# Storing gated convolution pieces one piece later in the out stage of a hybrid decoder layer

## The chip, the cores and the metric

The kernel runs on one core of a Trainium2 chip. The metric is the device time of one execution in microseconds (us). Five engines of the core matter here: PE (TensorE, matrix products), DVE (VectorE), ACT (ScalarE), POOL (GpSimd) and SP, whose queue issues most of the DMAs of this stage. Each works through its own list of instructions in order; an instruction whose data isn't ready holds everything behind it on that engine.

## The reference

One decoder layer is applied to a prompt of 2048 tokens and to 8 samples of 4 tokens. The input is normalised and projected, and its columns go to four groups of heads, each 512 wide; the outputs, gated, are concatenated, projected by `w_out` (2048 to 1024), normalised and added to the input.

```python
def conv_branch(a, b, hist, w_dw, b_dw, ln_g, ln_b, w_pw, b_pw):
    u = a * jax.nn.sigmoid(b)
    y = depthwise_conv31(concat([hist, u]), w_dw) + b_dw
    y = jax.nn.silu(layer_norm(y, ln_g, ln_b))
    y = y @ w_pw + b_pw                      # this step and the gate are
    ...                                      # what the change touches
y = concat([y_c * silu(gate_c), y_pool * ..., y_sb * ..., y_mem * ...]) @ w_out
out = x + rms_norm(y, post_g)
```

The other groups are a multi-scale pooling mixer, a stick-breaking attention (which for the samples reads a paged cache of 8192 tokens) and an attention over 256 memory tokens.

## The kernel before

The change lies in the last stage, "out", from about 1986 us to the end. Two streams of work are woven together there.

The first is the projection by `w_out`, made as seven Strassen-like products of half-size matrices in a fixed list (1, 7, then 2 and 6 mixed, then 4, 5 and 3). Each product has nine parts (eight of 256 tokens' worth of columns and one for the samples), each part two halves `h`. Both operands are fp32 split into a high and a low fp32r half, so a step takes three matmuls: `wohi` with `mh`, `wohi` with `ml`, `wolo` with `mh` (L1881, tile `acc`; 1408 matmuls in all). `out_part` yields after every quarter part. The right operand is read back from the mixture in DRAM (`mixd` for the prompt, `mixs` for the samples; loads `mr` at L1593 and L1610), combined on POOL (L1623), split on ACT (`mh`, L1635) and on DVE (`ml`, L1646). The weights are loaded raw (`wor`, L1514 and L1526), combined on POOL (L1536), written back to scratch for a later product (`wsd`, L1531) and split on ACT (`wohi`, L1542) and DVE (`wolo`, L1547). A finished `acc` is added into running sums on DVE (`U`, L1680 and L1681; `c`, L1684).

The second stream, `conv_post`, is the end of the convolution group. It takes the depthwise output in 8 blocks of 256 tokens (the last has 288, with the 32 sample tokens) and is a generator with these steps per block:

- `load` reads `cy`; `total` sums its four tiles on POOL (`cs`, L1372).
- `center`: PE makes the mean (`cm`, L1377), DVE subtracts it (L1380), ACT squares (`csq`, L1382), POOL adds the four squares (L1384).
- `scale`: PE makes the variance (`cv`, L1390), ACT and DVE its inverse root; for two tiles at a time DVE normalises (`ct`, L1399), ACT takes the sigmoid (`csg`, L1402), DVE multiplies (L1406), ACT and DVE split into `shi` (L1408) and `slo` (L1411).
- `gate` loads a gate piece into `cgt` (L1418), four pieces of 128 channels per block, three buffers.
- `point`, per piece: 12 matmuls `cz` (L1432) into one of two PSUM buffers, DVE's `cgt` = (cz + bias) * gate (L1435), and SP's store of the piece to `mixd` (L1437), for the last block also to `mixs` (L1439).

The main body steps `conv_post` once per 0.9 quarter parts (`OPACE`). After each block's pieces a flag ("conv", i) tells the other stream that its rows of the mixture may be read. Before it loads the weights of product 4, whose buffers lie in the convolution's memory, the main body runs `conv_post` to its end at one place of the list. PE's list is in program order; the lists of DVE, ACT, POOL and SP are ordered by a scheduler from the program's dependencies and so change with it.

## Time and profile before

| | |
|---|---|
| median of 3 runs | 2420.67 us (2417.32 to 2421.38) |
| profiled execution | 2424.11 us, span 2422.4 us |
| mean granted TensorE clock | 0.981 |
| PE busy | 2288.3 us, 94% of the span |
| DVE busy | 1720.1 us, 71% |
| POOL busy | 1301.5 us, 54% |
| ACT busy | 1116.8 us, 46% |
| bytes moved by DMA | 562.14 MB, mean 232 GB/s |

Busy is the share of the span in which an engine executes. In the lines of the profile shown below, a row of the timeline gives the start in us, the duration in us, engine, line, operation, output tile <- input tiles, partitions x elements with the type, and in brackets how long the engine had been idle and what released it. A row of the waits gives the waiting instruction, the releaser, the sum of the waits in us, their number and the longest. "SPq" is SP's queue of DMA issues; its row stands at the time of issue. "x2" behind a row means that two like instructions are merged in it.

### The profile page before, as it was taken

The numbers are of one execution on the slowest core, as the hardware profiler recorded it, in microseconds if no ns is written. First come the engines' busy times: TensorE is split into PE (matmuls) and PEld (weight loads), VectorE is DVE, ScalarE is ACT, GpSimd is POOL, SyncE is SP. The second block draws the span as 40 slices with busy tenths as digits, with TensorE's granted clock in tenths as the row PEclk, the third lists the DMA queues.
The fourth block names the chain that finished last, engine by engine and source line by source line (L and its number), as shares of the span: only waits on it lengthen the run. The fifth ranks groups of instructions, "written<-read, shape, count | busy, mean of one in ns | idle before, by whom it ended". The sixth has DMA issues, their size and how long they took to land. (4 is left out here: it accounts for less than half of the span.)

```text
span 2422.4 us, 42131 instructions
## 1 busy us (share of the span) xinstructions
PE 2288.3 (94%) x15962; PEld 1777.0 (73%) x15962; DVE 1720.1 (71%) x2410; ACT 1116.8 (46%) x1939; POOL 1301.5 (54%) x1333
## 2 busy tenths in 40 slices
PE   6999999999999999999999999899999998989997
PEld 6998888898888777777777776455555556778775
DVE  5333684968746665477777877888898846787898
ACT  5322343242442322224242425788989955443454
POOL 1553544555564455655555564576876845453431
PEclk9999999999999999999999999999999998999998
DMA  5678988877778799887877876834332227887764
GB/s 184 196 254 284 344 303 285 295 263 264 268 244 282 268 349 327 312 280 265 286 272 268 266 245 153 246 85 119 101 85 74 66 61 237 263 275 255 248 237 171
DMA packets 340438, 562.14 MB, mean 232 GB/s; under 512 B 28482, under 2 KB 212930, under 8 KB 323835
## 3 DMA queue, kind: packets, MB, share of 16 engines
q1 hardware_dynamic: 284858, 290.72, 39.1%
q0 software_dynamic: 55376, 268.72, 31.1%
q8 instruction: 126, 2.06, 0.3%
q14 instruction: 78, 0.63, 0.1%
HBM read 469.28 MB, written 90.68 MB: 231 GB/s over the span
## 5 line engine op out<-in xcount | busy, mean ns | idle before, releaser
L925 DVE STREAM_TRANSPOSE T<-kt 128x1024 f32<-128x1024 f32 x256 | 308.7, 1225 | 184.7 <-PE sSA L938 172.3
L892 POOL DMA_INDIRECT vt<-in_cache_v_dram,idv x256 | 251.3, 982 | 243.3 <-PE sO L977 182.3
L583 DVE SCALAR_TENSOR_TENSOR cacc<-U,par,cacc 128x512 f32<-128x512 f32 x480 | 360.0, 750 | 11.8
L1277 POOL TENSOR_TENSOR be<-be,E 128x512 f32<-128x512 f32 (+2 forms) x320 | 303.3, 955 | 115.4 <-DVE E L1268 49.4
L1268 DVE TENSOR_TENSOR_SCAN E<-gam,cr,ZM 128x513 f32<-128x513 f32 x192 | 232.8, 1262 | 15.3 <-ACT gam L1253 14.1
L892 POOL DMA_INDIRECT kt<-in_cache_k_dram,idk x128 | 125.6, 981 | 201.5 <-DVE T L925 141.0
L1288 PEld LDWEIGHTS AT<-ident,be 128*128 128x128 f32 x1088 | 116.7, 141 | 127.4 <-ACT at L1294 45.3
L1253 ACT ACTIVATE gam<-S,nbias_bc 128x1024 f32<-128x1024 f32 (+1 forms) x160 | 172.6, 1079 | 49.4 <-issue 18.5
L1881 PE MATMUL acc<-wohi,mh 128*128 128x512 f32 (+1 forms) x480 | 194.3, 405 | 0.9 <-ACT mh L1635 0.9
L1881 PE MATMUL acc<-wolo,mh 128*128 128x512 f32 (+1 forms) x480 | 190.9, 398 | 0.0
L1881 PE MATMUL acc<-wohi,ml 128*128 128x512 f32 x448 | 179.1, 400 | 10.0 <-DVE ml L1646 9.9
L1248 PE MATMUL S<-kT,Q 128*128 128x512 f32 (+1 forms) x640 | 176.4, 399 | 6.9 <-ACT be L1255 2.6
L1255 ACT ACTIVATE be<-S,bias_bc 128x1024 f32<-128x1024 f32 (+1 forms) x160 | 171.5, 1072 | 0.0
L1288 PE MATMUL AT<-ident,be 128*128 128x128 f32 x1088 | 157.0, 282 | 14.4 <-DVE at L1292 3.9
L1304 PE MATMUL av<-at,V 128*64 128x512 f32 (+3 forms) x640 | 152.6, 555 | 1.7 <-DVE sbo L1309 1.7
L938 PE MATMUL sSA<-T,W 128*32 128x128 f32 x4096 | 139.2, 277 | 6.8 <-DVE T L925 6.0
L938 PEld LDWEIGHTS sSA<-T,W 128*32 128x32 f32 x4096 | 104.7, 110 | 44.1 <-issue 37.4
L1646 DVE TENSOR_TENSOR ml<-mr,mh 128x512 fp32r<-128x512 f32 x108 | 100.2, 933 | 36.8 <-ACT mh L1635 36.6
L977 PE MATMUL sO<-vt,saT 128*32 128x512 f32 x1024 | 124.0, 598 | 0.0
L1248 PEld LDWEIGHTS S<-kT,Q 128*128 128x128 f32 x640 | 106.1, 194 | 23.2 <-ACT gam L1253 4.2
L1265 DVE TENSOR_TENSOR_SCAN E<-gam,ZM 128x128 f32<-128x128 f32 (+3 forms) x128 | 96.3, 801 | 29.6 <-ACT gam L1253 23.3
L1294 ACT COPY at<-AT 128x512 f32<-128x512 f32 x192 | 109.0, 656 | 14.4 <-PE AT L1288 14.4
(571 smaller groups left out, 6047.2 us busy)
## 6 DMA issues: line engine op xcount, KB each, us to landing
Q<-qd SPq DMA_DIRECT2D x64, 256.0 KB
mr<-mixd SPq DMA_DIRECT2D x32, 512.0 KB
mr<-mixd SPq DMA_DIRECT2D x48, 256.0 KB
wor<-in_w_out_dram SPq DMA_DIRECT2D x20, 512.0 KB
xtp<-in_x_prompt_dram SPq DMA_DIRECT2D x16, 512.0 KB
kT<-kd SPq DMA_DIRECT2D x64, 128.0 KB
wor<-in_w_out_dram SPq DMA_DIRECT2D x32, 256.0 KB
msd<-mr SPq DMA_DIRECT2D x32, 256.0 KB
```

Source lines behind the costliest of these rows:

```text
L583: dve.scalar_tensor_tensor(out=ps, in0=U[:, a + k : a + k + H], scalar=wd[:, k : k + 1], in1=ps, op0=ALU.mult, op1=ALU.add)
L892: pool.indirect_dma_start(out=dst, out_offset=None, in_=rows, in_offset=bass.IndirectOffsetOnAxis(ap=idx, axis=0))
L925: dve.transpose(T[:, 2 * hh : 2 * hh + 2].rearrange("p s j t -> p (s j t)"), kt[:, 2 * hh : 2 * hh + 2].rearrange("p s j d -> p (s j d)"))
L938: pe.matmul(sSs[n][32 * g : 32 * g + 32, P * ml : P * (ml + 1)], lhsT=W[:, jj, :], rhs=T[:, :, jj, :], start=i == 0, stop=i == 3, tile_pos ...
L1248: pe.matmul(S[:, j, :w], lhsT=Q[hh][:, x, P * (q2 + j) : P * (q2 + j + 1)], rhs=KT[hp, hh, kc][:, :w], start=x == 0, stop=x == 1)
L1253: act.activation(out=ga[:, :, 512 - w : 512], in_=S[:, :, :w], func=AF.Sigmoid, bias=nbias_bc[:, h : h + 1], scale=-1.0)
L1255: act.activation(out=be[:, :, :w], in_=S[:, :, :w], func=AF.Sigmoid, bias=bias_bc[:, h : h + 1])
L1268: dve.tensor_tensor_scan(out=E[:, j][:, ::-1], data0=ga[:, j][:, ::-1], data1=ZM[:, 0:1].to_broadcast([P, 513]), initial=carry[hh, q2][:, ...
L1277: pool.tensor_tensor(out=be[:, j, :m], in0=be[:, j, :m], in1=E[:, j, 513 - w : 513 - w + m], op=ALU.mult)
L1288: pe.transpose(ap_[:, P * qt : P * (qt + 1)], A[hp, qb, kc, hh, qt][:, P * r : P * (r + 1)], ident)
L1304: pe.matmul(av[64 * hh : 64 * hh + 64, c], lhsT=V[:, 4 * kc + r, 64 * hh : 64 * hh + 64], rhs=ats.pop((hp, qb, kc, r, hh))[:, c], start=dg ...
L1881: pe.matmul(o[:rows], lhsT=m[a][:, k, :rows], rhs=W[prod, 4 * h + k][w], start=not cont and h == k == n == 0, stop=h == 1 and k == 3 and n ...
```

## The change

Three things change in `conv_post`.

A piece's store isn't issued behind its own gating any more. It is put in a list `gated`, and `send(1)`, one turn of the generator after the piece, issues all but the newest; the block's last store is issued by `send(0)` behind the piece loop. The gate pieces get five buffers for three, in the pool `cpw`.

The additions of squares leave `center` for a step `squares`, at the seventh of the eleven turns between a block's start and its pieces.

Behind the pieces of a block, the first segment of the next block's `scale` (the matmul `cv`, the root and its inverse) is taken at once, followed by two more turns, and only then are the last store and the flag issued. A block so takes one turn more, 28 for 27.

```diff
--- before.py
+++ after.py
@@ -1356,7 +1356,11 @@
 
         CW = CB + NS
         blocks = [(a, a + CB) for a in range(0, SEQ - CB, CB)] + [(SEQ - CB, SEQ + NS)]
-        ys, sums, sqs, split, gates = {}, {}, {}, {}, {}
+        ys, sums, sqs, split, gates, gated = {}, {}, {}, {}, {}, []
+
+        def send(keep_):
+            while len(gated) > keep_:
+                wq.dma_start(*gated.pop(0))
 
         def load(i):
             if i < len(blocks):
@@ -1380,9 +1384,14 @@
                 dve.tensor_tensor(out=y[:, c, :N], in0=y[:, c, :N], in1=mps[:, :N], op=ALU.subtract)
                 sq.append(cp.tile([P, CW], F32, tag="csq", name=f"csq{a0}_{c}", bufs=4)[:, :N])
                 act.activation(out=sq[c], in_=y[:, c, :N], func=AF.Square)
-            for a, b in ((0, 1), (2, 3), (0, 2)):
-                pool.tensor_tensor(out=sq[a], in0=sq[a], in1=sq[b], op=ALU.add)
-            sqs[i] = sq[0]
+            sqs[i] = sq
+
+        def squares(i):
+            if i in sqs:
+                sq = sqs[i]
+                for a, b in ((0, 1), (2, 3), (0, 2)):
+                    pool.tensor_tensor(out=sq[a], in0=sq[a], in1=sq[b], op=ALU.add)
+                sqs[i] = sq[0]
 
         def scale(i):
             a0, N, y = blocks[i][0], blocks[i][1] - blocks[i][0], ys.pop(i)
@@ -1414,7 +1423,7 @@
 
         def gate(i, co):
             a0, a1 = blocks[i]
-            gates[i, co] = cp.tile([P, CW], F32, tag="cgt", name=f"cgt{a0}_{co}", bufs=3)
+            gates[i, co] = cpw.tile([P, CW], F32, tag="cgt", name=f"cgt{a0}_{co}", bufs=5)
             wq.dma_start(gates[i, co][:, : a1 - a0], gcd[co, :, a0:a1])
 
         def point(i):
@@ -1434,12 +1443,12 @@
                         n += 1
                 dve.scalar_tensor_tensor(out=g[:, :N], in0=ps[:, :N], scalar=par[:, co, CONV_K + 3 : CONV_K + 4],
                                          in1=g[:, :N], op0=ALU.add, op1=ALU.mult)
-                wq.dma_start(mix_rows(co, a0, CB), by_tile(g[:, :CB]))
+                gated.append((mix_rows(co, a0, CB), by_tile(g[:, :CB])))
                 if N > CB:
-                    wq.dma_start(mixs[0, :, co], g[:, CB:N])
-                yield
-                yield
-            flags.add(("conv", i))
+                    gated.append((mixs[0, :, co], g[:, CB:N]))
+                yield
+                send(1)
+                yield
 
         load(0)
         load(1)
@@ -1464,6 +1473,7 @@
             yield
             yield
         total(1)
+        squares(0)
         for _ in scale(0):
             yield
         for _ in range(4):
@@ -1474,11 +1484,18 @@
             if i + 1 < len(blocks):
                 center(i + 1)
                 side = scale(i + 1)
-            for _ in range(D2):
+            for k in range(D2):
+                if k == 6:
+                    squares(i + 1)
                 yield
             for _ in point(i):
                 yield
             total(i + 2)
+            next(side, None)
+            yield
+            yield
+            send(0)
+            flags.add(("conv", i))
             for _ in side:
                 yield
             for _ in range(D1):
```

What this does to the lists of the engines is shown at three places. A name as `wor_4` is a raw weight tile, `mr_1_0` a raw tile of the mixture (part 1, half 0), `cgt_2` gated piece 2; the number behind it is the build's own. Line numbers of the changed kernel are 4 to 17 above those of the kernel before; a store of a piece stands at L1363 there.

SP's list around the stores of the first block, before:

```order
L1437 DMA mixd<-cgt_0_20194 128x2x128
L1514 DMA wor_4_20218<-in_w_out_dram 128x2x512
L1514 DMA wor_5_20257<-in_w_out_dram 128x2x512
L1437 DMA mixd<-cgt_1_20281 128x2x128
L1418 DMA cgt_3_20343<-gcd 128x256
L1437 DMA mixd<-cgt_2_20312 128x2x128
L1593 DMA mr_0_0_20382<-mixd 128x2x512
L1593 DMA mr_0_1_20440<-mixd 128x2x512
L1437 DMA mixd<-cgt_3_20343 128x2x128
L1531 DMA wsd<-wor_4_20218 128x512
L1593 DMA mr_1_0_20473<-mixd 128x2x512
L1531 DMA wsd<-wor_5_20257 128x512
```

and now:

```order
L1531 DMA wor_4_20215<-in_w_out_dram 128x2x512
L1363 DMA mixd<-cgt_0_20194 128x2x128
L1531 DMA wor_5_20257<-in_w_out_dram 128x2x512
L1427 DMA cgt_3_20342<-gcd 128x256
L1363 DMA mixd<-cgt_1_20281 128x2x128
L1610 DMA mr_0_0_20380<-mixd 128x2x512
L1363 DMA mixd<-cgt_2_20311 128x2x128
L1363 DMA mixd<-cgt_3_20342 128x2x128
L1610 DMA mr_0_1_20430<-mixd 128x2x512
L1548 DMA wsd<-wor_4_20215 128x512
L1610 DMA mr_1_0_20473<-mixd 128x2x512
L1548 DMA wsd<-wor_5_20257 128x512
```

The raw weight 4 now stands ahead of the store of piece 0. The store of piece 3 follows the store of piece 2, and the second read of the mixture, `mr_0_1`, has moved behind it. Behind these rows follow, in both, the raw weight 6, a gate piece and the raw weight 7.

SP's list around the last block's stores, before:

```order
L1437 DMA mixd<-cgt_2_22197 128x2x128
L1439 DMA mixs<-cgt_2_22197 128x32
L1526 DMA wor_0_22303<-in_w_out_dram 128x512
L1526 DMA wor_0_22303<-wsd 128x512
L1437 DMA mixd<-cgt_3_22215 128x2x128
L1439 DMA mixs<-cgt_3_22215 128x32
L1526 DMA wor_1_22306<-in_w_out_dram 128x512
L1526 DMA wor_1_22306<-wsd 128x512
L1610 DMA mr_7_1_22294<-mixd 128x512
L1526 DMA wor_2_22328<-in_w_out_dram 128x512
L1686 DMA c11d<-c_5_22290 128x512
```

and now:

```order
L1363 DMA mixd<-cgt_0_22153 128x2x128
L1363 DMA mixs<-cgt_0_22153 128x32
L1363 DMA mixd<-cgt_1_22179 128x2x128
L1363 DMA mixs<-cgt_1_22179 128x32
L1363 DMA mixd<-cgt_2_22196 128x2x128
L1363 DMA mixs<-cgt_2_22196 128x32
L1363 DMA mixd<-cgt_3_22214 128x2x128
L1363 DMA mixs<-cgt_3_22214 128x32
L1627 DMA mr_7_1_22294<-mixd 128x512
L1543 DMA wor_0_22303<-in_w_out_dram 128x512
L1543 DMA wor_0_22303<-wsd 128x512
L1543 DMA wor_1_22306<-in_w_out_dram 128x512
```

The first raw weights of product 4 (`wor_0`, one half from the input and one from scratch) stood ahead of the store of piece 3; now they stand behind all eight stores and behind the read `mr_7_1`.

DVE's list in the last block, from the second half of `scale` to the first gating, before:

```order
L1406 TENSOR_SCALAR ct_0_22047<-ct_0_22047,par,csg_0_22049 128x288
L1406 TENSOR_SCALAR ct_1_22051<-ct_1_22051,par,csg_1_22053 128x288
L1411 TENSOR_TENSOR slo_22046<-ct_0_22047,shi_22045 128x288
L1411 TENSOR_TENSOR slo_22046<-ct_1_22051,shi_22045 128x288
L1399 TENSOR_SCALAR ct_2_22078<-cy_21590,par,cv_22038 128x288
L1399 TENSOR_SCALAR ct_3_22082<-cy_21590,par,cv_22038 128x288
L1646 TENSOR_TENSOR ml_5_1_22150<-mr_5_1_22057,mh_5_1_22149 128x512
L1406 TENSOR_SCALAR ct_2_22078<-ct_2_22078,par,csg_2_22080 128x288
L1406 TENSOR_SCALAR ct_3_22082<-ct_3_22082,par,csg_3_22084 128x288
L1680 TENSOR_TENSOR U_20001<-acc_4_22131,U_20001 128x512
L1411 TENSOR_TENSOR slo_22046<-ct_2_22078,shi_22045 128x288
L1411 TENSOR_TENSOR slo_22046<-ct_3_22082,shi_22045 128x288
```

and now:

```order
L1697 TENSOR_TENSOR U_19998<-acc_4_22123,U_19998 128x512
L1415 TENSOR_SCALAR ct_0_22088<-ct_0_22088,par,csg_0_22090 128x288
L1415 TENSOR_SCALAR ct_1_22092<-ct_1_22092,par,csg_1_22094 128x288
L1698 TENSOR_TENSOR U_19997<-acc_4_22123,U_19997 128x512
L1420 TENSOR_TENSOR slo_22087<-ct_0_22088,shi_22086 128x288
L1420 TENSOR_TENSOR slo_22087<-ct_1_22092,shi_22086 128x288
L1408 TENSOR_SCALAR ct_2_22105<-cy_21613,par,cv_22074 128x288
L1408 TENSOR_SCALAR ct_3_22109<-cy_21613,par,cv_22074 128x288
L1663 TENSOR_TENSOR ml_5_1_22275<-mr_5_1_22117,mh_5_1_22274 128x512
L1415 TENSOR_SCALAR ct_2_22105<-ct_2_22105,par,csg_2_22107 128x288
L1415 TENSOR_SCALAR ct_3_22109<-ct_3_22109,par,csg_3_22111 128x288
L1420 TENSOR_TENSOR slo_22087<-ct_2_22105,shi_22086 128x288
```

Ahead of the first two splits `slo` there is now the pair of operations `U` on an accumulator (`acc_4`); before, one of that pair stood between the second `ct` pair and the second splits. The order of the splits among themselves is as it was.

On PE the same 1408 `acc` matmuls and the same matmuls of the convolution are interleaved otherwise. Counted in `acc` matmuls that stand before it, piece 0 of blocks 0 to 7 stood at 138, 206, 277, 349, 424, 496, 568 and 640, and stands at 138, 208, 283, 358, 433, 508, 586 and 643; `cv` of block 7 stood at 589 and stands at 607.

## The prediction

> **What bounds the kernel now.** I read the page first, then each engine's busy time in the two stretches of the out stage, then the waits of TensorE and of the DMA queue in the first of them, then the timelines around the longest waits. Times are of the profiled execution: 2424.1 us, with a span of 2422.4. It lies 3.4 us above the median of 2420.67, so a sum made against it is shifted by that much at the end.
>
> ```profile
> span 2422.4 us, 42131 instructions
> PE 2288.3 (94%) x15962; PEld 1777.0 (73%) x15962; DVE 1720.1 (71%) x2410; ACT 1116.8 (46%) x1939; POOL 1301.5 (54%) x1333
> ...
> 1986.00:2226.00 240.00, 214.68 (x1061) 178.09 (x1060) 169.98 (x281) 113.22 (x223) 111.56 (x92) 0.94 0.78 250
> 2226.00:2405.00 179.00, 170.10 (x725) 133.47 (x724) 157.26 (x257) 89.71 (x227) 61.60 (x40) 0.99 0.70 239
> ```
>
> The last two lines are the out stage with the convolution in it, and without it: length, then PE, PEld, DVE, ACT and POOL busy, the granted clock, DMA share, GB/s. PE is idle 25.3 us of the first 240 at a clock of 0.94, and 8.9 of the second 179 at 0.99. Whatever the change can win lies in those 25.3 us and in the clock lost beside them. PE's waits there (line, releaser, sum, count, longest):
>
> ```profile
> PE cz L1432 <- DVE cgt L1435: 11.2, 4, 5.3
> PE cz L1432 <- ACT shi L1408: 9.4, 2, 8.1
> PE acc L1881 <- DVE ml L1646: 7.1, 6, 3.2
> PE cz L1432 <- DVE slo L1411: 2.4, 4, 1.0
> ...
> SPq L1437 <- DVE cgt L1435: 42.8, 23, 7.0
> POOL csq L1384 <- ACT csq L1382: 26.7, 8, 12.1
> ```
>
> The convolution's matmuls cz wait 23.0 us in all. Behind the first two lines stand the two queues that the change edits: SP waits 42.8 us with a gated piece's store at its head, everything behind it held, and POOL waits 26.7 us at the additions of squares.
>
> A long wait costs more than its length:
>
> ```profile
> 2010.43 0.39 PE L1881 MATMUL acc<-wohi,mh 128*128 128x512 f32 x1
> 2010.66 0.39 PE L1881 MATMUL acc<-wolo,mh 128*128 128x512 f32 x1
> ...
> 2252.26 0.50 PE L1881 MATMUL acc<-wohi,ml 128*128 128x512 f32 x1 [3.19 <-DVE ml L1646]
> 2253.24 0.63 PE L1881 MATMUL acc<-wohi,ml 128*128 128x512 f32 x1
> 2253.67 0.63 PE L1881 MATMUL acc<-wohi,mh 128*128 128x512 f32 x1
> ...
> 2135.00:2140.00 5.00, 3.05 (x18) 2.47 (x18) 4.86 (x7) 1.34 (x3) 4.38 (x4) 1.00 0.45 156
> 2145.00:2150.00 5.00, 4.83 (x17) 4.38 (x18) 2.79 (x5) 1.71 (x2) 2.36 (x2) 0.50 0.93 313
> ```
>
> Matmuls start 0.23 us apart in a full stream and 0.43 apart after a wait of 3.19; the clock reads 0.50 in the 5 us behind the wait of 5.26 shown below, and 1.00 around one of 1.92. Some 10 matmuls at half clock lose 2 us, which I add to each wait of 3 us or more. The Trainium skill ("TensorE: Matmul & The Clock Gate", part 1 on the HAM clock gate) has the clock halve after an idle window of about 3.4 us; the two windows agree, and the 3.19 lies a little under its figure.
>
> **The change, part by part.** It adds no matmul, load, store or byte; each of its costs is a place in an order. PE's order shifts because of one more turn per block: a quarter part of the output (3 acc matmuls) more stands before each later piece, so that piece 0 of the blocks 1 to 6 moves by 2 to 18 acc matmuls, 0.5 to 4.1 us. Those matmuls are issued in either case, and the shift alone costs nothing. Four edits have a price.
>
> *Block 0's stores and the weights behind them (gain).* The chain before:
>
> ```profile
> 2020.58 0.37 SPq L1437 DMA_DIRECT2D mixd<-cgt  x1
> 2021.04 1.27 SPq L1514 DMA_DIRECT2D wor<-in_w_out_dram  x2
> 2027.32 2.59 POOL L1536 TENSOR_TENSOR wor<-wor 128x512 f32<-128x512 f32 x2 [3.47 <-DMA wor<-in_w_out_dram]
> 2029.30 1.16 DVE L1547 TENSOR_TENSOR wolo<-wor,wohi 128x512 fp32r<-128x512 f32 x1 [6.08 <-ACT wohi L1542]
> 2031.71 0.36 SPq L1437 DMA_DIRECT2D mixd<-cgt  x1
> 2039.19 0.37 SPq L1514 DMA_DIRECT2D wor<-in_w_out_dram  x1
> 2044.17 1.26 POOL L1536 TENSOR_TENSOR wor<-wor 128x512 f32<-128x512 f32 x1 [2.07 <-DMA wor<-in_w_out_dram]
> 2045.46 0.62 ACT L1542 CAST wohi<-wor 128x512 fp32r<-128x512 f32 x1 [1.71 <-POOL wor L1536]
> 2047.74 0.58 PE L1432 MATMUL cz<-shi,pwhi 128*128 128x256 f32 x1 [8.11 <-ACT shi L1408]
> ```
>
> Piece 0's store holds the loads of the raw weights 4 and 5; their difference, split on ACT and DVE, stands before piece 3's gating on DVE; piece 3's store then holds the weights 6 and 7, whose split stands on ACT ahead of block 1's sigmoids, which cz waits for. The new order cuts this three times: weight 4's load goes ahead of the store, piece 3's gating comes ahead of the split of weight 5 on DVE, and the split of weight 7 goes behind block 1's last square on ACT. The blocked store costs SP at most 2031.71 − 2025.94 = 5.8 us (the load before it, below, ends at 2025.94). But SP still has the reads of the mixture and the write-backs of weights 4 and 5 ahead of weight 6, and they too wait for POOL. I take the 3.7 us by which weight 7's load can go earlier (piece 3 gated before the 1.16 of the split and 2.5 of its wait) and 1.3 of the half clock: **−5.0**, between 0 (the sigmoids arrive no earlier, since DVE is the limit) and −9.5 (the wait and most of its clock go).
>
> ```profile
> 2024.30 1.64 SPq L1593 DMA_DIRECT2D mr<-mixd  x2
> 2084.67 0.38 PE L1432 MATMUL cz<-shi,pwhi 128*128 128x256 f32 x1 [3.00 <-DVE cgt L1435]
> 2127.97 0.38 PE L1432 MATMUL cz<-shi,pwhi 128*128 128x256 f32 x1 [1.33 <-ACT shi L1408]
> 2136.86 0.39 PE L1432 MATMUL cz<-shi,pwhi 128*128 128x256 f32 x1 [1.92 <-DVE cgt L1435]
> 2145.17 0.58 PE L1432 MATMUL cz<-shi,pwhi 128*128 128x256 f32 x1 [5.26 <-DVE cgt L1435]
> ```
>
> *Blocks 2 and 4 (gain).* Block 2's piece 3 waits 3.00 us for a gating; it now stands six acc matmuls later, 1.4 us. POOL does the squares a little later and the weights' and mixture's sums a little earlier, which feed the same DVE: **−0.7**, between 0 and −2. Block 4's waits are 1.33, 1.92 and 5.26, plus about 2.6 at half clock. Nine matmuls more ahead of it (2.0 us) take away the first. The other two come from the gatings' place on DVE: before as after some fifteen operations stand between them, and two of the gatings now follow a difference of an accumulator that PE has yet to finish. **−2.5**, between −8 (all but the 1.92 goes) and +3 (one more such wait).
>
> *What is given back.* PE arriving earlier meets the same loads: the DMA share was 0.78 over the stretch, and DVE 71% busy, 88% in the next one. A gain can become a wait for the split ml of a later part. **+3**, between 0 and 5.
>
> *The last block (loss).* The products' next weights need the convolution's memory, so its last block is drained at one fixed place, after acc matmul 643 in both orders. With a turn more per block its statistics come later: from its cv to its first cz there were 51 acc matmuls, now 36, 8.2 us for 11.6. Before:
>
> ```profile
> 2207.78 0.94 DVE L1406 SCALAR_TENSOR_TENSOR ct<-ct,par,csg 128x288 f32<-128x288 f32 x2
> 2208.33 0.40 ACT L1408 CAST shi<-ct 128x288 fp32r<-128x288 f32 x1 [0.50 <-DVE ct L1406]
> 2209.36 0.69 DVE L1680 TENSOR_TENSOR U<-acc,U 128x512 f32<-128x512 f32 x1 [0.64 <-PE acc L1881]
> 2209.97 0.81 DVE L1411 TENSOR_TENSOR slo<-ct,shi 128x288 fp32r<-128x288 f32 x2
> 2210.47 0.40 PE L1432 MATMUL cz<-slo,pwhi 128*128 128x288 f32 x1 [0.23 <-DVE slo L1411]
> ```
>
> The accumulator of matmul 640 is taken by U on DVE; before, U stood ahead of the last two of the four splits only. Now two such U stand about the first two splits, and behind them DVE has both splits (0.81), two ct (0.94), one ml (taken as U, 0.69), two ct (0.94) and two splits (0.81) before the last quarter of cz can run. With 0.69 + 0.94 + 0.69 ahead, the last split ends about 6.5 us after matmul 640; PE would be there in 0.7 for matmul 643 and 1.2 for its first nine cz (288 of 512 columns each, at 0.23). A stall of 4.6, less the 0.23 there was, is +4.3 or so. It comes in pauses of 2 us or less, so I give the half clock a quarter of its price, +0.5: **+4.8**, between 3.5 and 6.5. By the skill's rule on the idle window named above, pauses that short leave the clock whole: it would be +4.3, and the sum 0.5 less.
>
> Behind it on SP, all four pieces and their sample columns (eight stores) and the read of the mixture that follows now stand ahead of the next product's first weights; before, those went ahead of piece 3's store.
>
> ```profile
> 2216.97 0.33 SPq L1526 DMA_DIRECT2D wor<-in_w_out_dram  x1
> 2217.64 0.52 DVE L1435 SCALAR_TENSOR_TENSOR cgt<-cz,par,cgt 128x288 f32<-128x288 f32 x1 [1.78 <-DMA cgt<-gcd]
> 2218.19 0.37 SPq L1437 DMA_DIRECT2D mixd<-cgt  x1
> 2221.43 0.32 SPq L1610 DMA_DIRECT2D mr<-mixd  x1
> ```
>
> The read waits for the stores to land: 2221.43 − 2218.19 = 3.2 us. The weights start 4.5 us later (2221.43 against 2216.97), less 1.0 of the 1.78 that piece 3 waited for its gate, which five buffers load earlier: **+3.5**. It is paid in the six waits for ml (7.1 us) that are there already, so it is between 0, if their cover lasts, and 5. The skill ("DMA: Bandwidth & Descriptors", anatomy of one DMA) puts the fixed cost of a transfer at about 2.0 us, mostly the write's receipt; the 3.2 here is longer, and by 2.0 the term would be +2.3.
>
> Sum: −5.0 − 0.7 − 2.5 + 3 + 4.8 + 3.5 = +3.1. Profiled 2427.2, so a median of 2427.2 − 3.4 = **2424** (2423.8).
>
> **The rivals.** *R1, the gains stay.* The DMA has room: the share is 0.78, and 0.45 where SP was blocked (the window 2135 to 2140). If stores no longer hold loads, block 1's wait goes nearly whole (−8.0), block 2's as above (−0.7), block 4's 5.26 goes (−5.4 with a little of its clock), nothing is given back, the last block costs its 4.3 and the weights 0.5: −9.3, median 2411. For it speaks that SP's 42.8 us are what the page shows as the releaser of those weights; against it, that DVE is the releaser of most of PE's waits and keeps its work.
>
> *R2, weight 7 comes no earlier (slower).* In the new order a read of the mixture goes behind piece 3's store and stands with weight 4's write-back and another read before weight 6. If SP waits there instead, the loads of weights 6 and 7 leave no earlier than 18.6 us after the first store (2039.19 − 2020.58), block 1 still waits about 8 and block 2 about 3; block 4 gets worse by its +3, and the end costs +4.8 + 3.5: +11.3, median 2432. It decides where that distance stays above 17. For it: SP's next reads take 1.64 a pair and depend on stores; against: weight 4's load now leaves first.
>
> *R3, it does nothing.* The waits that matter are set by the loads' bandwidth and the last block has its slack after all: 0, median 2420.7. Against it stands the fixed place of the drain, which nothing covers.
>
> **How the numbers follow.** My forecast 0.44, R1 0.28, R2 0.24, R3 0.04. A measurement of this kernel tells about 0.2%, 4.8 us, from no change. The forecast's own range, from its terms, is −3 to +9 (2417 to 2430): 0.22 of its 0.44 is slower by over 0.2%, 0.21 within, 0.01 faster. R1 is faster (0.28), R2 slower (0.24 at +11.3, nearly all), R3 same. Faster 0.29, same 0.25, slower 0.46. The range takes in both sides of R1 and R2 but for their outer fifth: 2408 to 2437.
>
> **What would show it.** Right: PE's 8.11 us wait before block 1's first cz shrinks to about 4, weights 6 and 7 leave SP some 3 us earlier after the first store; SP's wait on gated pieces falls from 42.8 us to under 20; the last block shows cz waits for slo summing to 4 us, and the first weights of the next product leave after the last store. Wrong: no cz wait over 1 us at the last block (that term too large), or block 1's first wait gone altogether (R1), or as long as before (R2). The ml waits after 2226 should grow from 7.1 to about 10; if they don't, the weights were covered.

## The result: 0.76% slower

The changed kernel takes 2439.06 us (median of 6 runs, 2436.06 to 2442.78), the kernel before 2421.03 (6 runs, 2413.05 to 2422.37). The ratio is 1.0076, with a 95% interval of 1.0061 to 1.0090: 18 us slower, 2 us above the end of the predicted range and beyond both rivals. The profiled execution of the changed kernel took 2438.94 us.

The page of the changed kernel, and its out stage in windows that begin 5 us earlier than before (the first `acc` matmul starts at 1960.0 here and at 1965.1 before):

```profile
span 2437.2 us, 42122 instructions
PE 2297.3 (94%) x15962; PEld 1785.2 (73%) x15962; DVE 1730.6 (71%) x2410; ACT 1116.6 (46%) x1939; POOL 1300.6 (53%) x1333
...
1981.00:2221.00 240.00, 212.05 (x1024) 176.95 (x1023) 172.53 (x276) 109.09 (x216) 109.72 (x90) 0.91 0.76 244
2221.00:2415.00 194.00, 182.33 (x760) 142.98 (x760) 162.02 (x253) 91.14 (x225) 63.13 (x42) 0.96 0.67 225
```

The engines' instructions are the same in number; PE is idle 28 us in the first 240 (25 before) at a clock of 0.91 (0.94), and the second window has grown from 179 to 194 us. The waits in the first window (the row of L1881 is the kernel before, in its window 1986 to 2226):

```profile
PE cz L1441 <- ACT shi L1417: 12.0, 4, 5.8
PE cz L1441 <- DVE cgt L1444: 7.6, 2, 6.6
PE acc L1898 <- DVE ml L1663: 6.5, 3, 3.0
PE acc L1881 <- DVE ml L1646: 1.1, 2, 0.9
...
SPq L1363 <- DVE cgt L1444: 41.7, 20, 6.5
POOL csq L1393 <- ACT csq L1386: 18.8, 8, 9.8
```

What the change was about hardly moved on SP (41.7 us for 42.8: a store still waits for its gating, there is only one matmul group more ahead of it) and fell by 8 us on POOL. Neither shows in the time. The waits for the split `ml` grew from 1.1 to 6.5 us; the 7.1 us of six waits that the prediction shows hold for a window up to 2300, and not for this one.

To see where the 18 us lie, the time that PE loses is worked out by place: the start of each matmul in the out stage, less 0.227 us for each `acc` matmul and 0.118 for each matmul of the convolution (`cz`, `cm`, `cv`) ahead of it. The difference between two points of the list is what was lost between them, waits and half clock together. Places are named by what is lost there; the numbers in brackets are `acc` matmuls.

| us lost | before | after | after again (e13) | pool (e1) | held weight (e9) | turn (e2) | late scale (e10) | stores (e3) | 27 turns, old pool (e16) |
|---|---|---|---|---|---|---|---|---|---|
| blocks 0, 1 (132 to 252) | 14.2 | 9.8 | 11.1 | 14.8 | 14.9 | 12.7 | 14.6 | 16.1 | 16.6 |
| block 2 (to 324) | 7.3 | 6.6 | 5.8 | 7.7 | 7.6 | 8.4 | 6.7 | 7.3 | 7.0 |
| blocks 3, 4 (to 480) | 15.8 | 22.5 | 22.1 | 16.1 | 15.1 | 27.2 | 17.2 | 17.2 | 16.2 |
| blocks 5, 6 (to 612) | 1.1 | 1.5 | 2.0 | 1.2 | 1.1 | 3.1 | 1.1 | 1.1 | 2.8 |
| last block (to 720) | 1.6 | 7.8 | 6.7 | 1.5 | 1.6 | 7.6 | 6.7 | 1.6 | 1.1 |
| product 4 (to 852) | 9.1 | 13.2 | 14.4 | 11.8 | 12.9 | 11.0 | 10.2 | 12.1 | 11.6 |
| rest (to the last) | 5.5 | 8.2 | 5.7 | 6.1 | 5.5 | 6.2 | 6.0 | 7.2 | 7.2 |
| behind the last matmul | 17.1 | 21.7 | 21.7 | 21.5 | 21.8 | 16.9 | 17.1 | 17.3 | 17.3 |

"After" and "after again" are one program: a row scatters by up to 2.5 us from run to run, but for the last block and the end, which repeat within about 1. (The rest scatters more: e5 and e14 below, again one program, lost 11.3 and 7.4 there.) The first `acc` matmul itself starts anywhere from 1957 to 1966 us in these profiles, of the same programs too; that scatter lies ahead of the stage and is why medians of several runs are needed.

Between before and after the stage lost 4.4 less at blocks 0 and 1, 0.7 less at block 2, and more at five places: blocks 3 and 4 (6.7), the last block (6.2), product 4 (4.1), the rest (2.7) and behind the last matmul (4.6). The rows sum to 19.6 us in these two profiles, for the 18 of the medians. Blocks 0 to 2 gained 5.1 for the 5.7 forecast there; the third gain that was forecast, at block 4, did not come. Taken apart at matmul 396, block 3 lost 7.5 for 0.8 (5.8 in e13), and block 4 15.0 for 14.9 (16.1 in e13): the new loss of this row is block 3's.

Block 3 has a wait that the kernel before did not have. The timelines of POOL, ACT and PE in the changed kernel:

```profile
2096.21 1.26 POOL L1640 TENSOR_TENSOR mr<-mr 128x512 f32<-128x512 f32 x1 [5.00 <-DVE U L1695]
2097.50 0.62 ACT L1652 CAST mh<-mr 128x512 fp32r<-128x512 f32 x1 [2.16 <-POOL mr L1640]
2098.44 0.58 PE L1441 MATMUL cz<-shi,pwhi 128*128 128x256 f32 x1 [3.43 <-ACT shi L1417]
```

ACT's cast `mh` (product 7, part 7, which PE needs at matmul 377) stands ahead of the splits that block 3 needs at 358, and waits for POOL. In block 4 PE waits 2.97 us for an `ml` at matmul 426 and 6.57 for a gating at 451. DVE between the two gatings around the longer wait:

```profile
2135.48 0.47 DVE L1444 SCALAR_TENSOR_TENSOR cgt<-cz,par,cgt 128x256 f32<-128x256 f32 x1
2137.40 1.12 DVE L1564 TENSOR_TENSOR wolo<-wor,wohi 128x512 fp32r<-128x512 f32 x1 [1.44 <-ACT wohi L1559]
...
2140.46 1.15 DVE L1663 TENSOR_TENSOR ml<-mr,mh 128x512 fp32r<-128x512 f32 x1 [0.74 <-ACT mh L1652]
2143.41 0.69 DVE L1564 TENSOR_TENSOR wolo<-wor,wohi 128x512 fp32r<-128x512 f32 x1 [1.80 <-ACT wohi L1559]
2144.02 0.68 DVE L1701 TENSOR_TENSOR c<-acc,U 128x512 f32<-128x512 f32 x1
...
2145.22 0.48 DVE L1444 SCALAR_TENSOR_TENSOR cgt<-cz,par,cgt 128x256 f32<-128x256 f32 x1
```

All three waits, 3.98 us, are for casts of ACT; the difference `c` does not wait. In the last block, and in the 3 us windows over it:

```profile
2208.13 0.40 PE L1441 MATMUL cz<-shi,pwhi 128*128 128x288 f32 x1 [0.96 <-ACT shi L1417]
2209.08 0.40 PE L1441 MATMUL cz<-slo,pwhi 128*128 128x288 f32 x1 [0.55 <-DVE slo L1420]
2211.76 0.61 PE L1441 MATMUL cz<-shi,pwhi 128*128 128x288 f32 x1 [1.75 <-ACT shi L1417]
...
2209.00:2212.00 3.00, 1.17 (x6) 0.94 (x6) 2.96 (x8) 1.55 (x4) 0.00 (x0) 0.77 0.37 143
2212.00:2215.00 3.00, 3.00 (x12) 2.79 (x13) 1.14 (x3) 0.14 (x1) 0.00 (x0) 0.50 0.02 5
2215.00:2218.00 3.00, 3.00 (x17) 3.00 (x15) 0.52 (x1) 0.00 (x0) 0.00 (x0) 0.59 0.19 49
```

There are three pauses, none over 1.75 us, and a clock of 0.77, 0.50 and 0.59 in the three windows. At half clock for 1.4, 3.0 and 2.5 us the windows would read just so: some 6.8 us from about 2210.6 on, within the third pause. Last, what DVE still has to do behind the last matmul, before and after (groups of its instructions from the last `acc` matmul on; the number of them stands behind the x):

```profile
L1736 DVE SCALAR_TENSOR_TENSOR oxt<-oxt,oss,gfin 128x1024 f32<-128x1024 f32 (+1 forms) x4 | 4.0, 1017 | 0.1
L1725 DVE SCALAR_TENSOR_TENSOR oxt<-acc,oss,oxt 128x512 f32<-128x512 f32 x3 | 2.2, 746 | 0.0
...
L1753 DVE SCALAR_TENSOR_TENSOR oxt<-oxt,oss,gfin 128x1024 f32<-128x1024 f32 (+1 forms) x5 | 5.3, 1069 | 0.1
L1742 DVE SCALAR_TENSOR_TENSOR oxt<-acc,oss,oxt 128x512 f32<-128x512 f32 x4 | 2.9, 745 | 0.0
```

The normalisation of the output's rows is one row tile further behind, and nothing covers it.

### The profile page after: what moved, and what is told of

Read it like the earlier page. It is cut to its first block, busy times and chain, and to the rows that moved or that the text cites. A ratio compares the mean times of both kernels' runs of the same rounds, so it can differ in the third digit from the quotient of the medians.

```text
span 2437.2 us, 42122 instructions
## 1 busy us (share of the span) xinstructions
PE 2297.3 (94%) x15962; PEld 1785.2 (73%) x15962; DVE 1730.6 (71%) x2410; ACT 1116.6 (46%) x1939; POOL 1300.6 (53%) x1333
## 5 line engine op out<-in xcount | busy, mean ns | idle before, releaser
L583 DVE SCALAR_TENSOR_TENSOR cacc<-U,par,cacc 128x512 f32<-128x512 f32 x480 | 360.2, 750 | 11.8
L1248 PEld LDWEIGHTS S<-kT,Q 128*128 128x128 f32 x640 | 106.2, 194 | 22.1 <-ACT be L1255 4.7
L1898 PEld LDWEIGHTS acc<-wohi,ml 128*128 128x128 f32 x448 | 86.7, 194 | 40.6 <-DVE ml L1663 21.1
```

The costliest lines, as they stand in the source:

```text
L583: dve.scalar_tensor_tensor(out=ps, in0=U[:, a + k : a + k + H], scalar=wd[:, k : k + 1], in1=ps, op0=ALU.mult, op1=ALU.add)
L1248: pe.matmul(S[:, j, :w], lhsT=Q[hh][:, x, P * (q2 + j) : P * (q2 + j + 1)], rhs=KT[hp, hh, kc][:, :w], start=x == 0, stop=x == 1)
L1898: pe.matmul(o[:rows], lhsT=m[a][:, k, :rows], rhs=W[prod, 4 * h + k][w], start=not cont and h == k == n == 0, stop=h == 1 and k == 3 and n ...
```

## The experiments: which edit costs what

The change has four edits: the pool and number of the gate buffers, the late stores, the added turn, and the squares' place. The first four kernels take the first three apart, and e12 has the last alone.

**e1, the pool alone.** `cgt` in the weights' pool, with its three buffers:

```diff
-gates[i, co] = cp.tile([P, CW], F32, tag="cgt", name=f"cgt{a0}_{co}", bufs=3)
+gates[i, co] = cpw.tile([P, CW], F32, tag="cgt", name=f"cgt{a0}_{co}", bufs=3)
```

> The kernel before with one edit: the three gate buffers are taken from the pool of the convolution's weights (cpw) and not from the convolution's own (cp). Nothing is stored later, no turn is added, three buffers as before. Theory A (the pool alone puts the first weights of product 4 behind the last block's stores, and orders DVE's end of the row normalisation later): the losses around acc matmuls 756 to 828 (+4), 1040 to 1290 (+3) and behind the last matmul (+4.6) appear here, while block 1's wait shrinks by some 4; net about +7, 2428. Theory B (these losses come from the stores being sent a piece later, or from the added turn): none of them here, and the time is 2417 to 2421.

Measured: 2427.79 for 2418.37, ratio 1.0041 (1.0025 to 1.0057). The end grew to 21.5 and product 4 to 11.8, as theory A has it; block 1 gained nothing, and the 3 us between matmuls 1040 and 1290 did not come. So the late weights of product 4, which the prediction put down to the stores, come without any store being late.

**e2, the turn alone.**

```diff
             total(i + 2)
+            next(side, None)
+            yield
+            yield
             for _ in side:
```

> The kernel before with one edit: behind a block's pieces the first segment of the next block's scale and two more turns, 28 turns for 27. Stores, pool, buffers and squares as before. Theory A: the turn alone brings the losses at block 3 (about acc matmuls 348 to 372, +6, since a read of the mixture's high half stands ahead of the splits on ACT) and at the last block (636 to 648, +6); the gain of block 1 in part (-2); nothing at 756 and behind the last matmul. Net +10, 2431. Theory B: it also brings the late losses, +18 or more, 2439.

Measured: 2436.97 for 2418.37, ratio 1.0074 (1.0051 to 1.0096). The turn alone costs as much as the whole change. The last block lost 7.6 and the end nothing, as theory A says; but blocks 3 and 4 lost 27.2, 23.9 of it at block 4, where PE's waits were for gatings. DVE there:

```profile
2139.01 0.47 DVE L1435 SCALAR_TENSOR_TENSOR cgt<-cz,par,cgt 128x256 f32<-128x256 f32 x1
...
2143.79 0.69 DVE L1687 TENSOR_TENSOR c<-acc,U 128x512 f32<-128x512 f32 x1 [3.70 <-PE acc L1884]
2145.83 0.69 DVE L1550 TENSOR_TENSOR wolo<-wor,wohi 128x512 fp32r<-128x512 f32 x1 [1.36 <-ACT wohi L1545]
...
2149.54 0.47 DVE L1435 SCALAR_TENSOR_TENSOR cgt<-cz,par,cgt 128x256 f32<-128x256 f32 x1
```

Between the gatings of two pieces stand a difference `c`, which waits 3.70 us for an accumulator of PE's, and a split that waits 1.36 for a weight. PE in turn waits 5.04 us for the second gating (and had waited 6.01 for the first). This is another picture than in the changed kernel, where the difference `c` did not wait.

**e3, the late stores alone**, with three buffers in the old pool and no turn:

```diff
-                wq.dma_start(mix_rows(co, a0, CB), by_tile(g[:, :CB]))
+                gated.append((mix_rows(co, a0, CB), by_tile(g[:, :CB])))
...
                 yield
+                send(1)
                 yield
...
+            send(0)
+            flags.add(("conv", i))
             total(i + 2)
```

> The kernel before with one edit: each piece's store is issued one turn behind the next piece, the last at the block's end. Three gate buffers in cp as before, no added turn, squares as before. Theory A: no loss at block 3, none at the last block, the first weights of product 4 stand ahead of the last store as before: within 3 us of before, 2418 to 2424. Theory B (late stores hold the weights of product 4 and the reads): +4 at acc matmuls 756 to 828 and +4 behind the last matmul, 2429.

Measured: 2422.02 for 2418.37, ratio 1.0011 (0.9996 to 1.0026): no change that can be told. Blocks 0 and 1 lost 16.1, so the late stores bring no gain there either, though the raw weights 6 and 7 left SP 13.2 and 16.2 us after the first store for 15.4 and 18.6 before. Product 4 lost 12.1 here, with its first weights still ahead of the last store.

**e4, the changed kernel with the old pool.**

```diff
-gates[i, co] = cpw.tile([P, CW], F32, tag="cgt", name=f"cgt{a0}_{co}", bufs=5)
+gates[i, co] = cp.tile([P, CW], F32, tag="cgt", name=f"cgt{a0}_{co}", bufs=3)
```

> The changed kernel with the gate buffers back as before: three, in cp. Late stores, added turn and moved squares stay. Theory A: the losses from matmul 756 on (4 + 3 + 4.6) go, those of block 3 and of the last block stay, and a part of block 1's gain goes: 2439 - 11 + 2 = 2430. Theory B: as the changed kernel, 2437 to 2441.

Measured: 2432.55 for 2418.37, ratio 1.0056 (1.0036 to 1.0076). The end is back at 17.5 and product 4 at 10.5. Blocks 3 and 4 lost 21.7 and blocks 0 and 1 12.7.

**e9, one load held back.** In the kernel before, the first raw weight of product 4 is made to follow the last store on SP:

```diff
-            sp.dma_start(t, wsd[q, j] if q < 2 else ...)
+            with tc.issue_after(shi_ins["store"].ins) if (prod, j) == (4, 0) else ExitStack():
+                sp.dma_start(t, wsd[q, j] if q < 2 else ...)
```

`shi_ins["store"]` is the store that was issued last (the lines that note it are left out here).

> The kernel before with one load held back on SP: the two DMAs of the first raw weight of product 4 go behind the last store of the last block, as the new pool has them; pool, buffers, stores and turns as before. Theory A (this one order is what the pool costs, and DVE's list at the end follows from it): the loss between 720 and 852 rises from 9.1 to about 12, the stretch behind the last matmul from 17.1 to 21.6, and the time by 7 to 9 to about 2428, as with the new pool alone. Theory C (the pool costs by its memory, waits for buffers): no change, 2419 to 2422.

Measured: 2429.33 for 2418.85, ratio 1.0045 (1.0032 to 1.0058), the same as the pool. SP's queue and DVE's groups behind the last matmul, in e9:

```profile
2214.86 0.37 SPq L1439 DMA_DIRECT2D mixd<-cgt  x1
2215.28 0.46 SPq L1441 DMA_DIRECT2D mixs<-cgt  x1
2215.84 0.40 SPq L1529 DMA_DIRECT2D wor<-in_w_out_dram  x1
...
L1739 DVE SCALAR_TENSOR_TENSOR oxt<-oxt,oss,gfin 128x1024 f32<-128x1024 f32 (+1 forms) x5 | 5.3, 1068 | 0.1
L1728 DVE SCALAR_TENSOR_TENSOR oxt<-acc,oss,oxt 128x512 f32<-128x512 f32 x4 | 2.9, 746 | 0.0
```

The weight leaves right behind the last store, product 4 loses 12.9, and the end shows the five and four operations of the changed kernel: 21.8. So the place of this one load is enough for what the pool costs: with it there the scheduler writes another list for DVE some 180 us later, in which a row tile's normalisation stands behind the last splits `ml`. That the two go together is shown; how the scheduler comes to the other list is not, nor why the pool puts the load there. At product 4 the loss is less clean: PE's waits for `ml` lie at other matmuls than in e1 (766, 790 and 838 for 778 to 814), and e3 lost as much there without it.

**e10, the last block alone.** Six idle turns ahead of the last block's `scale`, so that `cv` stands at 607 and the pieces at 643, all else in its place:

```diff
             total(i + 2)
+            for _ in range(6 if i == 6 else 0):
+                yield
             for _ in side:
```

> The kernel before with six idle turns ahead of the last block's scale, nothing else: its variance cv stands at acc matmul 607 and its pieces at 643, as in the changed kernel; all other blocks stay where they were. Theory A: the loss between 612 and 720 rises from 1.6 to 7.7, all other places as before, and the time by 6 to 2426. Theory C (the last block's loss comes from the late stores or from a queue that runs late since block 3): 2 or 3 there, 2421.

Measured: 2424.30 for 2418.85, ratio 1.0025 (1.0012 to 1.0039), 6.7 us lost at the last block and nothing else moved beyond scatter. The run-up from `cv` to the first piece thus makes this loss by itself. PE's waits there are those of the changed kernel to the hundredth:

```profile
2204.36 0.40 PE L1432 MATMUL cz<-shi,pwhi 128*128 128x288 f32 x1 [0.96 <-ACT shi L1408]
2205.30 0.40 PE L1432 MATMUL cz<-slo,pwhi 128*128 128x288 f32 x1 [0.55 <-DVE slo L1411]
2207.99 0.61 PE L1432 MATMUL cz<-shi,pwhi 128*128 128x288 f32 x1 [1.75 <-ACT shi L1408]
```

**e6, the last block forced half a part later** in the changed kernel:

```diff
-            yield at((2, 7, 0)) - 6
+            yield at((2, 7, 0)) - 5
```

> The changed kernel with the convolution's end forced half a part later (its last pieces stand behind acc matmul 652 for 643); all loads keep their place in the list. Theory A (the last block's loss is the distance between its variance cv and its first piece, 36 acc matmuls for 51): with 45 the stall falls by 2 us and its half clock goes, so the loss between 612 and 720 falls from 7.8 to about 4, and the next product's weights start up to 2 us later: 2436. Theory C (the wait moves with the drain, since the accumulators' U stand between the splits wherever it is): 7 to 8 again, 2439.

Measured: 2433.61 for 2420.15, ratio 1.0055 (1.0035 to 1.0075); the last block lost 5.4 for 7.8, between the two theories. Of the 2 us of more run-up one came back: the pauses fell from 3.3 to 2.3 us (1.73 and 0.55). The clock still fell to half behind them.

**e7, 27 turns in the changed kernel:**

```diff
-D1 = 3
+D1 = 2
```

> The changed kernel with D1 = 2 for 3, so that a block takes 27 turns as before; everything else of the change stays (late stores, five buffers in the new pool, squares, the first segment of scale behind the pieces). Theory A: the turn's losses at block 3 and at the last block go (6.7 + 6.2), those of the pool stay (product 4, behind the last matmul): 2439 - 13 = 2426. Theory C (it is the place of cv, taken at once behind the pieces, that costs, not the count): 2435 or more.

Measured: 2426.98 for 2420.15, ratio 1.0027 (1.0014 to 1.0040). Blocks 3 and 4 lost 16.5, the last block 1.1, and blocks 0 and 1 lost 17.4: with the turn's losses its gain went too. The end stayed at 21.7.

**e16, both undone** (the edits of e4 and e7 together); late stores, squares and the early first segment of `scale` stay.

> The changed kernel with both costs undone: three gate buffers in the old pool, and D1 = 2 so that a block takes 27 turns. What stays are the late stores, the squares' place and the first segment of scale ahead of the last store. Theory A (pool and turn count are the whole loss): 2420 plus or minus 3, no loss at block 3, the last block, matmul 720 to 852 or the end. Theory D (late stores cost by themselves): 2425 or more.

Measured: 2426.12 for 2423.38, ratio 1.0007 (0.9993 to 1.0021). The kernel before was slower too when timed beside it, so the ratio decides between the theories: pool and turn count are the whole loss that can be measured.

**e12, the squares alone:**

```diff
-            for a, b in ((0, 1), (2, 3), (0, 2)):
-                pool.tensor_tensor(out=sq[a], in0=sq[a], in1=sq[b], op=ALU.add)
+        def squares(i):
+            ...
-            for _ in range(D2):
+            for k in range(D2):
+                if k == 6:
+                    squares(i + 1)
                 yield
```

> The kernel before with the additions of squares alone moved behind the sixth turn of a block. Both theories: no place moves by over 1.5 us, 2418 to 2422; a gain of over 4 us would say that POOL's wait at the squares had held the sums behind them.

Measured: 2419.37 for 2418.85, ratio 1.0004 (0.9994 to 1.0014). POOL's waits at the squares cost nothing before, and moving them brings nothing.

**e11, the turn behind block 0 only:**

```diff
             total(i + 2)
+            if i == 0:
+                next(side, None)
+                yield
+                yield
             for _ in side:
                 yield
-            for _ in range(D1):
+            for _ in range(D1 - (i == 1)):
                 yield
```

> The kernel before with the added turn behind block 0 only, and one idle turn less behind block 1, so that only block 1 moves (its pieces to 208 to 223, as in the changed kernel). Theory A (the turn, not the stores, brought the gain of block 1): the loss of blocks 0 and 1 together falls from about 15 to 12.5, everything behind as before, 2417. Theory C (the gain needs the earlier stores and weights): 15 again, 2420.

Measured: 2419.08 for 2418.85, ratio 0.9998 (0.9985 to 1.0011). Blocks 0 and 1 lost 12.9, and block 3, whose place is as before, lost 4.6 for 0.8: what PE gained was given back at the next wait. No version faster than the kernel before came of it.

**e8, ACT's cast of weight 7 held behind block 1's splits** in the kernel before, one half of what was to bring the gain at block 1:

```diff
-        act.copy(hi, ts[0])
+        with tc.issue_after(shi_ins[1].ins) if (prod, j) == (7, 7) else ExitStack():
+            act.copy(hi, ts[0])
```

`shi_ins[i]` is block i's last split `shi`, here and below (the lines that note it are left out).

> The kernel before with one instruction held back on ACT: the cast of weight 7's high half (product 7, needed by PE at acc matmul 230) behind block 1's last split shi (needed at 206). Theory A (ACT's order is what block 1's wait of 8 us hangs on): the loss between 180 and 252 falls from 12.7 to 9 or less as in the changed kernel, 2415. Theory C (DVE or the loads are late all the same): 12 again, 2419 to 2421.

Measured: 2420.43 for 2420.15, ratio 0.9998 (0.9986 to 1.0010). Block 1 lost 10.4 for 12.7, block 0 3.1 for 1.6: within scatter nothing.

**e5 and e14, ACT's cast ahead of block 3's splits held back** in the changed kernel, and **e13**, the changed kernel beside it.

```diff
-        act.copy(mh[:, :, :rows], raws[x])
+        with tc.issue_after(shi_ins[3].ins) if x == (7, 7, 0) else ExitStack():
+            act.copy(mh[:, :, :rows], raws[x])
```

> The changed kernel with one instruction held back on ACT: the high half of the mixture for product 7, part 7, half 0 (needed by PE at acc matmul 377) is issued behind the last of block 3's splits shi (needed at 358), as it is in the kernel before. Theory A (ACT's order is block 3's cause): the loss between acc matmuls 324 and 396 falls from 7.5 to under 3, and the time by about 6 to 2433. Theory C (the loss is PE's earlier arrival at loads that land when they land): the wait only moves, 7 us of loss remain by matmul 396, 2437 to 2440.

> The changed kernel as it is, timed beside the next three on one chip: 2437 to 2441 by every theory; its losses by place show how far a place moves from run to run of one program.

> The changed kernel with the one cast held behind block 3's splits, as in the earlier run where the loss of block 3 fell from 7.5 to 3.6 and the time did not. Theory A (that was a run's scatter in the late waits): 4 us under the changed kernel beside it, 2435. Theory D (the 4 us are given back behind, since DVE and the loads arrive no earlier): the same time as the changed kernel within 1.5 us.

Measured: e5 2439.77 (1.0079, 1.0061 to 1.0097); timed at another time, e13 2439.73 (1.0072, 1.0050 to 1.0093) and e14 2439.91 (1.0070, 1.0052 to 1.0087). PE in e14:

```profile
2099.42 0.39 PE L1443 MATMUL cz<-shi,pwhi 128*128 128x256 f32 x1 [0.65 <-ACT shi L1419]
...
2109.61 0.38 PE L1443 MATMUL cz<-shi,pwhi 128*128 128x256 f32 x1 [2.10 <-DVE cgt L1446]
...
2128.56 0.50 PE L1901 MATMUL acc<-wohi,ml 128*128 128x512 f32 x1 [4.16 <-DVE ml L1666]
```

The wait for block 3's splits (2.77 in e13) shrinks to 0.65, and two others take its place: one for a gating, 2.10, and one for a split `ml`, 4.16 for the 2.67 of e13. Blocks 3 and 4 together lost 21.8 (19.4 in e5) for the 22.1 of e13: block 3 less, block 4 more. The row of ACT that looked like the cause is not what the time hangs on.

**e15, the turn alone with two casts held**, the edit of e14 and:

```diff
-        act.copy(hi, ts[0])
+        with tc.issue_after(shi_ins[4].ins) if (prod, j) == (6, 5) else ExitStack():
+            act.copy(hi, ts[0])
```

> The kernel before with the added turn, and two casts on ACT held behind the splits: the mixture's of product 7 part 7 behind block 3's, weight 5's of product 6 behind block 4's. With the turn alone blocks 3 and 4 lost 27.2 for 15.8. Theory A (ACT's order is the loss): 17 to 19, time 2437 - 9 = 2428. Theory D (the gatings wait on DVE behind differences of accumulators that PE has yet to finish, whatever ACT does): 25 or more, 2434 to 2438.

Measured: 2442.17 for 2423.38, ratio 1.0074 (1.0055 to 1.0093); blocks 3 and 4 lost 24.8, with waits of 5.98 and 5.63 for gatings, and between these gatings DVE's difference `c` again waited 3.52 us for an accumulator. These two casts are not what the turn's loss hangs on. That the place of the gatings on DVE sets it, as theory D has it, fits, but no run moved a gating.

## Why the prediction was wrong

Two steps failed: blocks 3 and 4 were priced as a gain of 2.5, all of it block 4's and block 3's move at nothing, and lost 6.7 more; and the list of DVE behind the last matmul was left out of the sum, where 4.6 was lost. Term by term:

- **Block 1, −5.0: right in size, wrong in cause.** Blocks 0 and 1 lost 4.4 less. But late stores, earlier weights and the cast's place bring nothing (e3 16.1, e16 16.6, e8 13.5, before 14.2); all eight profiles with the full turn lie between 9.8 and 13.3, and the nine with no turn added between 13.5 and 17.4. So the gain comes with the turn. The chain that was read from SP through POOL, DVE and ACT is in the trace, yet acting on it brought no smaller loss; the prediction had named this as the bound "0, since DVE is the limit". That the size came out is luck.
- **Block 2, −0.7: as it came.**
- **Block 4, −2.5, and block 3, at nothing: the step that failed first.** Block 4 was taken as a gain, with +3 as the other end, and came out even (15.0 for 14.9). Its waits of 1.33 and 1.92 went, but 2.97 for an `ml` came at matmul 426, and the 5.26 for a gating became 6.57. The text saw that two of the gatings follow an accumulator's difference; in the changed kernel these differences do not wait, and DVE waits for ACT's casts. They wait where the turn stands with the old pool (3.70 us in e2, 3.52 in e15, 2.71 in e4), and there later matmuls don't help, since the accumulator comes later with them. Block 3 moves as far as block 4, nine matmuls, was not priced at all, and lost the 6.7. That the turn brings this loss is shown (27.2 with it alone, 16.5 and 16.2 without it in e7 and e16); which chain sets it stays open, since the wait that e14 undid only moved.
- **Given back, +3:** 2.7 between 852 and the end, but the repeat of the same program shows 0.2, so this is scatter and neither right nor wrong. The wait for `ml` at 426 is of the kind that the term names, but it lies in block 4's row.
- **The last block, +4.8: right** (6.2 and 5.1 in the two runs, 5.1 in e10 by itself). The pauses sum to 3.3 us for the 4.6 worked out, with only 0.55 of them for `slo`, and the half clock makes the rest, some 3 us: half a microsecond for it was too low. That pauses this short leave the clock whole, as the rule of the Trainium skill ("TensorE: Matmul & The Clock Gate", part 1 on the HAM clock gate) was read, did not hold: the clock is 0.50 behind them. The total came near because one part was too high and the other too low.
- **Product 4's weights, +3.5: right in size** (4.1; 5.3 in e13, 3.8 in e9), wrong in the edit: the pool, not the stores, puts them there (e1, e3). That this place is the whole of the row's loss is not shown: the late stores leave the weights where they were and lose 12.1 there by themselves (e3; 11.6 in e16). The read that stood ahead of them did not wait for the 3.2 us that were carried over from before, but less:

```profile
2220.87 0.37 SPq L1363 DMA_DIRECT2D mixd<-cgt  x1
2221.28 0.47 SPq L1363 DMA_DIRECT2D mixs<-cgt  x1
2222.74 0.32 SPq L1627 DMA_DIRECT2D mr<-mixd  x1
2223.18 0.37 SPq L1543 DMA_DIRECT2D wor<-in_w_out_dram  x1
```

  From the store's issue to the read's it is 2222.74 − 2220.87 = 1.9 us. The Trainium skill ("DMA: Bandwidth & Descriptors", anatomy of one DMA) has a fixed cost of about 2.0 us, there for DMAs that GpSimd issues; these are SP's, and come near it.
- **The end, +4.6: missing from the sum.** The prediction compared the orders around the convolution and not DVE's list behind it, where the number of operations behind the last split rises from 27 to 34. It could be read from the order alone. With the pool or the held load it is there (21.5 to 21.8), without them it is not (16.9 to 17.5).

Of the signs named ahead, the weights of product 4 did leave after the last store. PE's wait before block 1's first `cz` fell from 8.11 to 5.84 us (5.18 in e13), and not to about 4; weights 6 and 7 left SP 14.2 and 17.5 us after the first store for 15.4 and 18.6, about 1 us earlier and not 3; SP's wait for gated pieces did not fall. The waits for `ml` behind the first window went from 8.8 us in seven to 9.8 in seven.

With +0.1 at block 4, +6.7 at block 3 and +4.6 at the end, the forecast's sum would be 3.1 + 2.6 + 6.7 + 4.6 = 17.0, near the 18 measured; it still holds the +3 that no run shows. The rivals failed too: R1 kept gains that don't come from the stores. R2 gave block 1 no gain, where there was one, and put its loss at block 4 and behind; it came nearer than the forecast (2432), without block 3 or the end. None had the pool as a mechanism, or the turn anywhere but at the last block.

Pool and turn don't add: 0.41% and 0.74% alone, 0.76% for the whole change, and taking out the pool is worth 0.2% of it (e4) and the turn 0.5% (e7). In the table the turn alone loses 4.7 more at blocks 3 and 4 and 2.9 more at blocks 0 and 1 than the whole change does. At blocks 3 and 4 it is not the pool that spares this: e4, with the old pool and three buffers, lost 21.7 there. So the late stores or the squares' place do; open stays which, since no run parts them beside the turn. At blocks 0 and 1 e4 lost 12.7, as the turn alone did, and the five profiles with turn and new pool 9.8 to 11.7: there pool and buffers spare some 2 us, and whether it is the pool or the number of buffers stays open too.

## What to carry to other kernels

Compare the orders to the very end of the program, and not only around the edit: a scheduler that reacts to one load writes another list far behind it, and one more operation chain behind the last matmul is paid in full. Where two streams are woven by counts, price a count that is added per block at the place where the count is forced to end, and at every wait whose releaser moves along with PE; a matmul that comes later gives no slack to an operation that waits for matmuls (the difference `c` in e2). And undo a wait before calling its releaser the cause: here the most visible new wait was worth nothing, since two others stood behind it.

## What the runs showed of the hardware

The clock fell to half at pauses of 0.96, 0.55 and 1.75 us that lay within 4.6 us, PE being busy 1.17 of the 3 us from 2209 to 2212; it read 0.50 in the 3 us behind and 0.59 in the next 3. A single wait of 1.92 us left it at 1.00 before. The same program with the same three pauses, in e13, over its last block:

```profile
2209.00:2212.00 3.00, 1.33 (x6) 0.89 (x6) 3.00 (x8) 1.37 (x4) 0.00 (x0) 1.00 0.90 258
2212.00:2215.00 3.00, 1.52 (x5) 1.31 (x6) 2.30 (x5) 1.32 (x4) 0.00 (x0) 0.74 0.13 50
2215.00:2218.00 3.00, 3.00 (x18) 3.00 (x17) 0.70 (x2) 0.00 (x0) 0.00 (x0) 0.69 0.21 55
```

Here 0.74 and 0.69 make 1.56 + 1.86 = 3.4 us at half clock, for 6.8 above, and the block lost 6.7 for 7.8. The clock records of all 18 traces show why, in the stage from 1990 to 2400 us: each of the 116 stretches at half clock is 3.41 us long or two, three or four times that. Laid on the grid of 3.41 us that they mark, each fall followed a window of the grid in which PE idled 1.48 us or more, in one wait or in several; no window with over 1.85 us of idle time left a full clock full. (Between the two figures both happen; the ends of matmuls are modelled.) So several short waits together can cost what one long wait does, their price is not read from the longest, and it depends on where the grid happens to lie.
